# Two PSUM banks in turn for the delta rule's products, and the second head group's v transposed a step ahead

## The chip, the cores and the metric

The program runs on one core of one Trainium2 chip. The metric is the device time of one execution in microseconds (us). A measurement is the median of several runs; lower is better.

## The reference

It is one inference step of a decoder trunk of two layers, for a prompt of 2048 tokens and a group of 8 sample rows, in fp32. The even layer is attention beside pooling; the odd layer is a gated delta rule of 6 heads beside a spatial gate, and only its prompt part is touched here. The 2048 tokens are cut into chunks; a state s of 128x128 per head goes from chunk to chunk:

```python
def step(s, xs):
    q_c, k_c, u_c, w_c, g_c, a_c = xs
    delta = u_c - jnp.einsum('bhcd,bhdv->bhcv', w_c, s)
    o = jnp.einsum('bhcd,bhdv->bhcv', q_c * jnp.exp(g_c)[..., None], s) + jnp.einsum('bhij,bhjv->bhiv', a_c, delta)
    g_last = g_c[..., -1:]
    s = s * jnp.exp(g_last)[..., None] + jnp.einsum('bhcd,bhcv->bhdv', k_c * jnp.exp(g_last - g_c)[..., None], delta)
    return s, o
```

Here `u_c` and `w_c` come from v and k through the inverse of a triangular matrix of each chunk. The outputs are the two residual streams and the new caches and states.

## The kernel before

The odd layer works on two halves of 1024 tokens. In each half the main flow is made of matmul blocks: the input projection with its convolution (`conv_silu`, PSUM tiles cv), the gates and the output projection (`out_tile`, tiles acc). A large product is made as three matmuls in fp32r (`mm3`, L193 to L195: high by high, low by high, high by low). The delta rule of a half is a generator, `delta`; the main flow calls `tick` between its blocks, and each tick writes some more of the recurrence into the program at a high priority. The Tile framework's scheduler then sets the order on each engine by operands, buffers and priority. This order is fixed in the program: an engine works its own list from the top.

A half has 8 chunks of 128 tokens by 2 head groups (g = 0 and 1, three heads each), that is 16 items. Each item goes through stages with the lags of `DORD` (L50): load (q, k and the decay row gb), front (transposes of k and q, decay matrix A, products of k and q; L1338 to L1368), and then, per chunk with both groups together, blocks (inverse of 16x16 blocks on VectorE, with small loads and stores), merge16 and merge (inverses merged up to the matrix U of 128x128 a head; merge16 also loads v, L1434). Then comes step (L1497), which is the recurrence, and out (the output is transposed and stored).

The step of an item with state S is, by line:

- L1508: three transposes of v by TensorE; L1509: VectorE multiplies them by s, giving vt.
- L1512: ScalarE makes Sd, the decayed S.
- L1515: p1 = k·S; L1517: VectorE makes r = vt − p1.
- L1520: p2 = U·r; L1522: VectorE makes e from it.
- L1525 and L1526: output po = q·S + A·e. L1529: p3 = k·e; L1530: VectorE writes S = Sd + p3.
- L1533 to L1536: o is normalised (squares on ScalarE, power on GpSimd, multiplication on VectorE); L1544 to L1547: o is transposed, copied and stored.

PSUM has eight banks. `bank()` (L81) gives each product a tile of the kind that it names, and `OD` (L55) lists the banks that a kind takes in turn: the step's v transposes, p1, p2 and p3 are of kind rr (bank A); po is do, the output's transposes are oo (both bank B); front's products and the sample's are fr and side (bank C); the merges are dm (the two buffers Y). acc and cv use X (two buffers), X and D in the main. A product waits until the tile that held its bank before has been read.

```python
OD = dict(acc="XXD", fr="C", dm="Y", rr="A", do="B", oo="B", side="C", gv0="XXDYYAB", gv1="XXD", cv0="XXDYYAB", cv1="XXD")
```

All DMAs are issued by SyncE. In the second half the sample's own delta rule is mixed into the same stretch (L1575 to L1662). The run ends with the output projection of the last token tile, which needs the last item's o.

Of the kernel before, what the change touches and what calls it, by code (L numbers as in the profile page):

```python
# [15 lines left out]
ALU = mybir.AluOpType  # L16
# [4 lines left out]
P = 128  # L21
# [30 lines left out]
CM = 1  # L52
BQ, QB, GB, AB = 1, 5, 1, 4
PRIO = dict(delta=1000)
OD = dict(acc="XXD", fr="C", dm="Y", rr="A", do="B", oo="B", side="C", gv0="XXDYYAB", gv1="XXD", cv0="XXDYYAB", cv1="XXD")  # L55
PB, TB = 9, 6
W0 = 4, 4, 2
WT = 0
# [5 lines left out]
class Net:  # L64
# [1017 lines left out]
    def odd(self):  # L1082
        nc, I, O = self.nc, self.I, self.O
        st = ExitStack()
        self.banks = dict(OD, h=OD["acc"])
        self.odd_consts(st)
# [199 lines left out]
    def delta(self, half, gt, dl):  # L1286

        pairs = [dict(half=half, t=t) for t in range(8)]
        items = [dict(half=half, t=t, g=g, pair=pairs[t]) for t in range(8) for g in range(2)]
        stages = dict(load=self.delta_load, front=self.delta_front, blocks=self.delta_blocks, merge16=self.delta_merge16,  # L1290
                      merge=self.delta_merge, step=self.delta_step, out=self.delta_out)
        for i in range(len(items) + 6):

            for j, lag in DORD:
                if 0 <= i - lag < len(items):
                    x = items[i - lag]
                    pair = j in ("blocks", "merge16", "merge")
                    if not pair or x["g"]:
                        stages[j](x["pair"] if pair else x, gt, dl)
                        if j != "load":  # L1300
                            yield
# [156 lines left out]
    def delta_merge(self, y, gt, dl):  # L1458
# [31 lines left out]
        for x in y["gs"]:  # L1490
# [3 lines left out]
                mm(pu[:H, i, :], xx[H:, i, :H], U[H:, i, H:], start=True, stop=True)  # L1494
            nc.scalar.mul(U[:H, :, H:], pu[:H], -1.0)

    def delta_step(self, x, gt, dl):  # L1497

        nc = self.nc
        mm = nc.tensor.matmul  # L1500
        k, q, kt, A, U = (x[n] for n in ("k", "q", "kt", "A", "U"))
        g, c0 = x["g"], x["c0"]
        S = self.S[g]
        b3 = lambda a: a[:, :, None].broadcast_to([P, 3, P])
        v, vt = x["v"], self.d3(dl, "vt", 2)
        pt = self.bank("rr", 3, P)
        for i in range(3):
            nc.tensor.transpose(pt[:, i, :], v[:, i, :], self.ident)  # L1508
        nc.vector.tensor_tensor(vt, pt, b3(x["s"]), ALU.mult)  # L1509
        Sd = self.d3(dl, "Sd", 2)  # L1510
        for i in range(3):
            nc.scalar.mul(Sd[:, i, :], S[:, i, :], x["el"][:, i:i + 1])  # L1512
        p1 = self.bank("rr", 3, P)
        for i in range(3):
            mm(p1[:, i, :], k[:, i, :], S[:, i, :], start=True, stop=True)  # L1515
        r = self.d3(dl, "re", BR)
        nc.vector.tensor_tensor(r, vt, p1, ALU.subtract)  # L1517
        p2 = self.bank("rr", 3, P)
        for i in range(3):
            mm(p2[:, i, :], U[:, i, :], r[:, i, :], start=True, stop=True)  # L1520
        e = self.d3(dl, "re", BR)
        nc.vector.tensor_tensor(e, p2, b3(x["c"]), ALU.mult)  # L1522
        po = self.bank("do", 3, P)
        for i in range(3):
            mm(po[:, i, :], q[:, i, :], S[:, i, :], start=True, stop=False)  # L1525
            mm(po[:, i, :], A[:, i, :], e[:, i, :], start=False, stop=True)  # L1526
        p3 = self.bank("rr", 3, P)
        for i in range(3):
            mm(p3[:, i, :], kt[:, i, :], e[:, i, :], start=True, stop=True)  # L1529
        nc.vector.tensor_tensor(S, Sd, p3, ALU.add)  # L1530
        o, ss = self.d3(dl, "o", BO), dl.tile([P, 3], F32, tag="oss", name="oss", bufs=2)
        for i in range(3):
            nc.scalar.activation(o[:, i, :], po[:, i, :], AF.Square, scale=P ** -0.5, accum_out=ss[:, i:i + 1])  # L1533
        nc.vector.tensor_tensor(ss, ss, x["qe"], ALU.add)
        self.rstd(ss, 0.0)
        nc.vector.tensor_tensor(o, po, b3(ss), ALU.mult)  # L1536
        x["o"] = o
# [247 lines left out]
```

## Time and profile before

| | us |
|---|---|
| median of 3 runs | 3079.72 |
| lowest and highest of them | 3072.3, 3086.37 |
| profiled execution | 3071.84 |
| its span in the trace | 3070.1 |
| TensorE (PE) busy | 2787.3 |
| VectorE (DVE) busy | 2083.2 |
| GpSimd (POOL) busy | 1669.2 |
| ScalarE (ACT) busy | 1491.4 |

The profiled execution is one run; its span goes from the first to the last instruction of the trace. PEld is TensorE's weight load, which lies beside its matmuls; SPq is the queue of SyncE that issues the DMAs. The trace names tiles by their names in the program (rr, do, vt), and lines of kernel.py as L1508. PEclk is the granted clock of TensorE as a share of full speed; its mean over the run is 0.966.

### The profile page before, as it was taken

The page shows a single profiled execution, that of the slowest core. Times are in us where ns is not written, and L with a number is a line of the kernel's source. Part 1 is how long each engine was busy: PE and PEld are TensorE (multiplying, and loading weights), DVE is VectorE, ACT ScalarE, POOL GpSimd, SP SyncE. Part 2 cuts the span into 40 slices and gives each one's busy share as a digit, 9 for nine tenths or more (in the row PEclk, how much of TensorE's full clock was granted, in tenths as well). Part 3 has the DMA queues.
Part 4 walks back from the last instruction along what each step waited for, and adds up shares of the span by engine and source line. Part 5 has one row for each costly group of instructions (what it writes and reads, how often), then busy time and mean ns, then how long its engine had stood idle before and what let it go on. Part 6 is the DMA issues. An engine that isn't in the chain of part 4 may idle for free. (4 is left out here: it accounts for less than half of the span.)

```text
span 3070.1 us, 57853 instructions
## 1 busy us (share of the span) xinstructions
PE 2787.3 (91%) x20425; PEld 2534.0 (83%) x20425; DVE 2083.2 (68%) x4067; ACT 1491.4 (49%) x4431; POOL 1669.2 (54%) x1223
## 2 busy tenths in 40 slices
PE   8999899999998889989897988989999888778999
PEld 8999798899777777778787888878989878667887
DVE  5464455554898989894588777567888564567562
ACT  6644245534787778772222324445554533454331
POOL 4576546562567776674576665454444253255541
PEclk9999899999999999999999999999999999999999
DMA  4567866556344333307676665434333333467543
GB/s 162 160 206 245 254 209 200 192 180 181 104 100 110 93 84 100 73 28 237 212 256 201 201 192 179 130 112 139 106 92 97 94 84 113 134 180 219 146 122 99
DMA packets 428062, 462.55 MB, mean 151 GB/s; under 512 B 84988, under 2 KB 338341, under 8 KB 427773
## 3 DMA queue, kind: packets, MB, share of 16 engines
q1 hardware_dynamic: 427772, 458.86, 50.3%
q8 instruction: 162, 2.65, 0.4%
q14 instruction: 128, 1.04, 0.1%
HBM read 332.41 MB, written 126.33 MB: 149 GB/s over the span
## 5 line engine op out<-in xcount | busy, mean ns | idle before, releaser
L193 PE MATMUL acc<-bh,whi 128*128 128x256 f32 (+4 forms) x1208 | 405.2, 336 | 11.2 <-DVE cx L1244 4.6
L195 PE MATMUL acc<-bh,wlo 128*128 128x256 f32 (+4 forms) x1208 | 402.5, 334 | 3.7 <-DVE wlo L901 3.4
L194 PE MATMUL acc<-bl,whi 128*128 128x256 f32 (+4 forms) x1208 | 402.1, 333 | 2.0 <-DVE bl L882 2.0
L822 ACT ACTIVATE p<-sc,nb 128x512 f32<-128x512 f32 (+3 forms) x480 | 302.1, 642 | 76.0 <-DVE nb L821 63.7
L845 POOL TENSOR_TENSOR p<-p,cf 128x512 f32<-128x512 f32 (+3 forms) x240 | 236.9, 1006 | 182.4 <-ACT p L822 46.4
L635 POOL TENSOR_TENSOR kp<-kp,at 128x768 f32<-128x768 f32 x120 | 207.9, 1741 | 163.6 <-DMA kp<-in_cache_v 145.6
L821 DVE TENSOR_REDUCE nb<-sc 128x1 f32<-128x512 f32 (+3 forms) x480 | 275.6, 597 | 19.4 <-PE sc L820 10.3
L195 PE MATMUL cv<-bh,wlo 128*128 128x346 f32 (+2 forms) x864 | 283.6, 329 | 3.2 <-POOL wlo L174 2.3
L193 PE MATMUL cv<-bh,whi 128*128 128x346 f32 (+2 forms) x864 | 284.3, 329 | 1.4 <-DVE th L429 1.0
L194 PE MATMUL cv<-bl,whi 128*128 128x346 f32 (+2 forms) x864 | 284.4, 329 | 0.0
L174 POOL TENSOR_TENSOR wlo<-wraw,whi 128x1024 fp32r<-128x1024 f32 (+1 forms) x90 | 216.7, 2411 | 117.3 <-ACT whi L172 117.1
L557 POOL TENSOR_TENSOR kp<-kp,qb 128x768 f32<-128x768 f32 x88 | 167.3, 1907 | 180.0 <-DMA kp<-in_cache_k 137.6
L193 PEld LDWEIGHTS acc<-bh,whi 128*128 128x128 f32 (+1 forms) x1208 | 231.6, 192 | 27.8 <-issue 5.6
L193 PE MATMUL acc<-whi,bh 128*128 128x256 f32 x864 | 250.6, 290 | 0.2 <-DVE th L425 0.2
L194 PE MATMUL acc<-wlo,bh 128*128 128x256 f32 x864 | 249.2, 289 | 1.4 <-POOL wlo L174 1.4
L195 PE MATMUL acc<-whi,bl 128*128 128x256 f32 x864 | 249.0, 288 | 0.0
L195 PEld LDWEIGHTS acc<-bh,wlo 128*128 128x128 f32 (+1 forms) x1208 | 231.4, 192 | 20.4 <-DVE wlo L901 4.6
L194 PEld LDWEIGHTS acc<-bl,whi 128*128 128x128 f32 (+1 forms) x1208 | 231.4, 192 | 15.7 <-DVE bl L882 2.5
L859 PE MATMUL pv<-v,pt 128*128 128x128 f32 x1632 | 218.1, 281 | 16.7 <-ACT pt L857 9.8
L817 PE MATMUL sc<-kh,q 128*128 128x512 f32 (+2 forms) x480 | 210.0, 438 | 25.1 <-ACT p L822 21.0
L859 PEld LDWEIGHTS pv<-v,pt 128*128 128x128 f32 x1632 | 201.3, 194 | 31.4 <-ACT junk L862 13.9
L637 DVE TENSOR_TENSOR sacc<-sacc,kp 128x768 f32<-128x768 f32 x120 | 176.0, 1467 | 73.6 <-POOL kp L635 64.8
(445 smaller groups left out, 8449.8 us busy)
## 6 DMA issues: line engine op xcount, KB each, us to landing
kp<-in_cache_k SPq DMA_DIRECT2D x128, 384.0 KB
kp<-in_cache_v SPq DMA_DIRECT2D x128, 384.0 KB
wraw<-in_w_in_e SPq DMA_DIRECT2D x56, 512.0 KB
wraw<-in_w_in_o SPq DMA_DIRECT2D x56, 512.0 KB
mc<-cat SPq DMA_DIRECT2D x72, 256.0 KB
mg<-sg SPq DMA_DIRECT2D x72, 256.0 KB
kh<-kh SPq DMA_DIRECT2D x48, 256.0 KB
kl<-kl SPq DMA_DIRECT2D x48, 256.0 KB
```

Source lines behind the costliest of these rows:

```text
L174: e.tensor_tensor(lo, raw, hi.bitcast(F32), ALU.subtract)
L193: mm(out, ah, bh, start=first, stop=False)
L194: mm(out, ah, bl, start=False, stop=False)
L195: mm(out, al, bh, start=False, stop=last)
L557: (nc.vector if j % 3 == 2 else nc.gpsimd).tensor_tensor(k, k, qb, ALU.mult)
L635: nc.gpsimd.tensor_tensor(h3(w), h3(v), self.at[:, b, j, :, None].broadcast_to([P, NH, P]), ALU.mult)
L637: nc.vector.tensor_tensor(acc, acc, v, ALU.add)
L817: mm(sc[:, :w], qc, kh[:, c, :w], start=True, stop=False)
L821: nc.vector.tensor_reduce(nb[:, c, j:j + 1], sc[:, :n], AX.X, ALU.max, negate=True)
L822: nc.scalar.activation(p[:, c, :n], sc[:, :n], AF.Exp, bias=nb[:, c, j:j + 1], accum_out=l[:, c, j:j + 1])
L845: nc.gpsimd.tensor_tensor(p[:, 1, :n], p[:, 1, :n], cf[:, 1, j:j + 1].broadcast_to([P, n]), ALU.mult)
L859: mm(pv, tt[:, t, :], kvt[j][2][:, t, :], start=j == 0 and t == 0, stop=j * 4 + t == nk - 1)
```

## The change

The kind rr takes the banks A and Y in turn, so p1, p2 and p3 of the steps alternate between A and one of the two buffers that the merges use. The transposes of v and the multiplication that makes vt become a function of their own, `delta_v`, with a kind of its own on bank C. Each item knows the next one; after a step has written S, it calls `delta_v` for the next item if that item's v is loaded. Since merge16 loads v for both groups of a chunk together, this is so for the step of group 0 (the next item is group 1 of the same chunk); group 0 of the next chunk still makes its vt at the head of its own step.

```diff
-OD = dict(acc="XXD", fr="C", dm="Y", rr="A", do="B", oo="B", side="C", gv0="XXDYYAB", gv1="XXD", cv0="XXDYYAB", cv1="XXD")
+OD = dict(acc="XXD", fr="C", dm="Y", rr="AY", vt="C", do="B", oo="B", side="C", gv0="XXDYYAB", gv1="XXD", cv0="XXDYYAB", cv1="XXD")
...
+        for x, y in zip(items, items[1:] + [{}]):
+            x["next"] = y
...
+    def delta_v(self, x, dl):
+
+        nc = self.nc
+        x["vt"] = vt = self.d3(dl, "vt", 2)
+        pt = self.bank("vt", 3, P)
+        for i in range(3):
+            nc.tensor.transpose(pt[:, i, :], x["v"][:, i, :], self.ident)
+        nc.vector.tensor_tensor(vt, pt, x["s"][:, :, None].broadcast_to([P, 3, P]), ALU.mult)
+
     def delta_step(self, x, gt, dl):
...
-        v, vt = x["v"], self.d3(dl, "vt", 2)
-        pt = self.bank("rr", 3, P)
-        for i in range(3):
-            nc.tensor.transpose(pt[:, i, :], v[:, i, :], self.ident)
-        nc.vector.tensor_tensor(vt, pt, b3(x["s"]), ALU.mult)
+        if "vt" not in x:
+            self.delta_v(x, dl)
+        vt = x["vt"]
...
         nc.vector.tensor_tensor(S, Sd, p3, ALU.add)
+        if "v" in x["next"]:
+            self.delta_v(x["next"], dl)
```

In the changed file the lines have other numbers: v transposes L1505, p1 L1524, q·S L1534, A·e L1535, p3 L1538, output transposes L1555; merge16's first product is L1442 instead of L1440, the q transposes L1357 instead of L1355.

The first place is TensorE's order in the first half, at the step of a second head group. S_20770 and S_20771 are the states of the two groups; T and cm are operands of merge16. Before:

```order
L1440 MATMUL dm<-T,cm 128x128 x3
L1355 MATMUL fr<-ident,qk 128x128 x3
L193 MATMUL cv_27911<-bh,whi 128x352
L194 MATMUL cv_27911<-bl,whi 128x352
L195 MATMUL cv_27911<-bh,wlo 128x352
L193 MATMUL cv_27911<-bh,whi 128x352
L1526 MATMUL do<-re,A 128x128
L1525 MATMUL do<-S_20771,qk 128x128
```

Now:

```order
L195 MATMUL cv_27995<-bh,wlo 128x346
L1538 MATMUL rr<-re,kt 128x128 x3
L1524 MATMUL rr<-S_20770,qk 128x128 x3
L1534 MATMUL do<-S_20771,qk 128x128
L1535 MATMUL do<-re,A 128x128
L193 MATMUL fr<-qh 128x256
L194 MATMUL fr<-cm,qh 128x256
L195 MATMUL fr<-qh,cm 128x256
```

The product p3, which came behind q·S and A·e, now stands ahead of them, with p1 of the next group right behind it; the merge's product, which came ahead of them, now follows 48 rows later.

The second place is TensorE's order at the start of the second half's recurrence, at its first transposes of q. Before:

```order
L195 MATMUL cv_30322<-bh,wlo 128x346
L1355 MATMUL fr<-ident,qk 128x128 x3
L1508 MATMUL rr<-ident,v 128x128 x3
L193 MATMUL cv_30322<-bh,whi 128x346
L194 MATMUL cv_30322<-bl,whi 128x346
```

Now, where the front stage's products of that item stand:

```order
L195 MATMUL cv_30356<-bh,wlo 128x352
L193 MATMUL fr<-qh 128x256
L194 MATMUL fr<-cm,qh 128x256
L195 MATMUL fr<-qh,cm 128x256
```

The v transposes have left this place for one 674 matmuls later; the first instruction here that needs another engine's work is then the product of the front stage, 39 matmuls behind where the v transposes were.

The third place is the end of TensorE's order, at the last output transposes. Before:

```order
L195 MATMUL acc<-bh,wlo 128x512
L193 MATMUL acc<-bh,whi 128x512
L1544 MATMUL oo<-ident,o 128x128 x3
L194 MATMUL acc<-bl,whi 128x512
L195 MATMUL acc<-bh,wlo 128x512
```

Now:

```order
L194 MATMUL acc<-bl,whi 128x256
L195 MATMUL acc<-bh,wlo 128x256
L1555 MATMUL oo<-ident,o 128x128 x3
L193 MATMUL acc<-bh,whi 128x256
L194 MATMUL acc<-bl,whi 128x256
L195 MATMUL acc<-bh,wlo 128x256
```

They moved 23 matmuls towards the end of the order: 30 instead of 53 are left between them and the first product of the last tile.

## Rows read from the trace of the kernel before

**Rows 1.** the page's busy time of each engine: us, share of the span, instructions

```profile
PE 2787.3 (91%) x20425; PEld 2534.0 (83%) x20425; DVE 2083.2 (68%) x4067; ACT 1491.4 (49%) x4431; POOL 1669.2 (54%) x1223
```

**Rows 2.** windows; columns: us, PE, PEld, DVE, ACT, POOL busy, PEclk, DMA share, GB/s

```profile
2100.00:2435.00 335.00, 324.14 (x2778) 306.79 (x2779) 260.89 (x639) 178.56 (x563) 150.62 (x114) 1.00 0.34 102
2435.00:2455.00 20.00, 10.46 (x58) 10.18 (x57) 7.90 (x21) 7.37 (x27) 2.84 (x3) 0.75 0.50 130
2500.00:2550.00 50.00, 32.03 (x208) 26.92 (x209) 26.72 (x62) 9.91 (x23) 32.31 (x17) 0.76 0.31 62
2625.00:2720.00 95.00, 68.58 (x470) 59.86 (x470) 49.38 (x122) 40.53 (x148) 39.41 (x25) 0.92 0.55 149
```

**Rows 3.** PE's waits, 1935 to 3071: awaited line, us in total, times, longest

```profile
PE side L1599 <- DVE arena L1596: 11.0, 1, 11.0
PE rr L1508 <- DMA v<-y: 9.5, 1, 9.5
...
PE rr L1508 <- DVE S L1530: 6.8, 5, 2.5
PE rr L1515 <- DVE vt L1509: 6.8, 4, 4.0
...
PE oo L1544 <- DVE o L1536: 4.5, 5, 1.7
...
PE do L1526 <- DVE re L1522: 3.0, 2, 2.6
```

**Rows 4.** groups of instructions, whole run: busy us, mean ns | idle before, releaser

```profile
L1509 DVE TENSOR_TENSOR vt<-rr,ks 128x384 f32<-128x384 f32 x32 | 17.5, 546 | 2.1 <-PE rr L1508 2.1
...
L1508 PE MATMUL rr<-ident,v 128*128 128x128 f32 x96 | 17.0, 283 | 16.5 <-DMA v<-y 9.5 <-DVE S L1530 6.8
```

**Rows 5.** PE's waits, 2625 to 2720

```profile
PE rr L1515 <- DVE vt L1509: 5.4, 2, 4.0
...
PE rr L1508 <- DVE S L1530: 2.5, 1, 2.5
```

**Rows 6.** DVE's waits, 2625 to 2720

```profile
DVE s L1647 <- DMA s<-sdd: 32.8, 10, 6.0
```

**Rows 7.** timeline at the stall of 2441: start us, us, instruction [idle before, releaser]

```profile
2439.73 0.32 PE L193 MATMUL cv<-bh,whi 128*128 128x346 f32 x1
...
2440.21 0.31 PE L193 MATMUL cv<-bh,whi 128*128 128x346 f32 x1
...
2441.16 0.49 PE L1355 MATMUL fr<-ident,qk 128*128 128x128 f32 x3
...
2447.43 0.37 SPq L1434 DMA_DIRECT2D v<-y  x1
...
2450.70 1.00 POOL L1338 TENSOR_TENSOR A<-gb,dmask 128x384 f32<-128x384 f32 x1 [15.65 <-DMA gb<-grow]
...
2451.18 0.90 PE L1508 MATMUL rr<-ident,v 128*128 128x128 f32 x3 [9.54 <-DMA v<-y]
...
2451.74 0.98 ACT L1340 ACTIVATE A<-A,nG 128x128 f32<-128x128 f32 x3 [10.26 <-POOL A L1338]
...
2454.93 0.20 ACT L1357 ACTIVATION_READ_ACCUMULATOR N<-fr 128x1 f32 x1
```

**Rows 8.** timeline and chain of waits at the end of the run

```profile
3039.22 0.56 DVE L1536 TENSOR_TENSOR o<-do,oss 128x384 f32<-128x384 f32 x1 [0.96 <-POOL oss L126]
...
3044.31 0.49 PE L1544 MATMUL oo<-ident,o 128*128 128x128 f32 x3
...
3045.50 2.15 DMA cat<-o
...
3053.62 0.50 PE L193 MATMUL acc<-bh,whi 128*128 128x512 f32 x1 [1.98 <-ACT whi L900]
...
3058.54 0.12 PE acc L194
...
3058.78 0.23 PE acc L193
```

## The prediction

> **What bounds the kernel now.** I read the page first, then the windows of the second half of the run, then TensorE's waits there, then the timeline of the two longest stalls, and last the chain that ends the run. The page says TensorE: it is busy 2787.3 us, 91% of the span, and no other engine passes 2083.2 [rows 1]. The delta recurrence, the only code that is changed, runs from about 1935 us on, so only that part can give anything back. The windows [rows 2] show it in two kinds. In the long stretch 2100 to 2435 TensorE is busy 324.14 of 335.00 us at a granted clock of 1.00: all its idle time together is 10.9 us. Holes stand at 2435 to 2455 (10.46 of 20.00 busy, clock 0.75), 2500 to 2550 (32.03 of 50.00, clock 0.76) and 2625 to 2720 (68.58 of 95.00, clock 0.92).
>
> What TensorE waits for in that part [rows 3] divides into what the change can reach and what it cannot. It can reach the v transposes waiting for bank A (they wait for S, because the group before still holds the bank: 6.8 us in 5 waits), k·S waiting for vt (6.8 us in 4), and one wait of the v transposes for the load of v (9.5 us). It cannot reach the longest wait of all, 11.0 us of the sample's own matmuls on DVE. That makes 6.8 + 6.8 + 9.5 = 23.1 us, 0.8% of the run, as everything that stands in front of the changed instructions today.
>
> **The change, part by part.**
>
> *Work.* The count stays: 32 steps with three transposes of v each (96 matmuls, 283 ns each) and one multiplication by s (32 of 546 ns) [rows 4]. Nothing is added on TensorE, DVE or a queue, so this costs nothing by itself. The results go to the front stage's bank C in place of A. On GpSimd nothing moves past anything. On SP the loads of v keep their place; only one small load of the block stage stands behind a store, and nothing waits for it at once. I take 0, with the 2.15 us of one store [rows 8] as the upper bound and nothing below.
>
> *The wait for S behind the v transposes.* For the second head group the transposes now stand ahead of the group before, on another bank; for the first group they stand on C too. So the 6.8 us of waits for S go, but 2.5 of them lie at 2625 to 2720 [rows 5]. There the recurrence is mixed with the sample's state updates, and DVE, which must make vt, e and S in its own order, waits 32.8 us in 10 waits for loads of the sample's state [rows 6]. Taking a bank wait out ahead of that leaves the next instruction waiting for the same DVE. I count 6.8 − 2.5 = 4.3 us as gained.
>
> *The wait for vt behind k·S.* 6.8 us in 4 waits, but 5.4 of them in that same stretch [rows 3, 5], and with the same reason they move on. I count 1.4 us.
>
> *The hole at 2441.* After the q transposes at 2441.16 TensorE stands for 9.54 us in front of the v transposes; their load was issued at 2447.43 [rows 7]. In the changed order the first v transposes of this half stand 674 matmuls later, so this wait goes. What is late next? TensorE goes on with 39 products of the convolution at 0.16 us each (three of them between 2439.73 and 2440.21) and then comes to the products of the front stage, which write bank C over the q transposes. ScalarE must read those first, and its reads stand in its queue behind the exponentials of A, which wait for GpSimd's A at 2450.70 (1.00 us), itself 15.65 us behind a load. ScalarE starts the exponentials at 2451.74 and ends its last read at 2455.13 [rows 7]; that chain is untouched by the change. So TensorE stops at about 2441.65 + 39 × 0.16 = 2447.9 and stays until the chain is done, which also runs the other small reads of the front stage: to about 2455.6, by my estimate from these rows. The stall is then 7.7 us in place of 9.5: a gain of about 2. The bounds are nothing and the whole 9.5 us, plus at most 0.25 × 20.00 = 5.0 us of clock, since the window was granted 0.75 [rows 2]. I take 2, by the rows of ScalarE.
>
> *The pair of banks.* The recurrence now alternates between A and the two buffers Y that the merges use. That takes away waits of one product for the read-out of the one before, but it adds two. A merge product that takes a Y buffer stands behind the read of S of the second group; and S may not be overwritten before q·S has read it, while q·S needs bank B, which the output transposes of the group before still hold. Neither wait is in the trace in that form. The nearest rows are the output transposes waiting for o (4.5 us in 5 waits, longest 1.7) and the product of e waiting for its operand (3.0 in 2) [rows 3]. Spread over all 32 steps the first is 4.5 / 32 = 0.14 us. If every one of 32 steps paid the mean of a wait, 4.5 / 5 = 0.9 us, it were 28.8 us. Below nothing: 4.5 + 3.0 us, if a quicker recurrence takes these waits away as well. I take 0.14 for each of the 16 steps of the second group, 2.2 us lost, since in 2100 to 2435 TensorE has matmuls of the convolution and the gates to do meanwhile and the merges' operands come early.
>
> *The end.* The run's last chain goes from the last S and o through the last output transposes, the store and the load of the mixed tile to the last product [rows 8]. o is ready at 3039.22 + 0.56, but TensorE, in its fixed order, comes to the transposes only at 3044.31: their place in the order, not o, sets the start. In the changed order they stand 23 matmuls later (with 30 and not 53 left until the wait for the last tile). Five of these have 512 columns at 0.23 us and 18 have 256 at 0.12 [rows 8]: 5 × 0.23 + 18 × 0.12 = 3.3 us later, all of it on the path, since after it TensorE waits for that chain in both (1.98 us for ScalarE's weights there). I count 3.3 lost.
>
> *Sum.* −4.3 − 1.4 − 2.0 + 2.2 + 3.3 = −2.2 us. Against the profiled execution's own 3071.84 that is 3069.6. That execution was 7.9 us under the median 3079.72 of the three runs, so I forecast **3077 us**. About 0.5% (15.4 us) is what a measurement of this kernel can tell from no change, so this is no change.
>
> **Rivals.**
>
> *Faster: all waits on the changed path go, and nothing takes their place.* 6.8 + 6.8 + 9.5 and 5.0 of clock, less 3.3 at the end: −24.8 us, 3055 by the median. For it: the recurrence is one serial chain, the order now puts three more independent matmuls ahead of it, and the waits are seen. Against it: the two places with the largest share have their next wait already in the rows [rows 6, 7]. The Trainium skill, Perfetto Trace Analysis, Matmuls, says that independent groups of matmuls should rotate through several PSUM banks so that reading one overlaps the next one's products. By that rule this rival would hold; the trace agrees only so far that the waits on bank A exist, and they are 13.6 us without the load of v [rows 3]. 0.24.
>
> *Slower: bank B becomes the loop's end.* p3 of the second group now stands ahead of q·S, and S waits for q·S, which waits for the chain squares, power, o, output transposes, copy on bank B. If each of the 16 second steps lost (0.9 + 1.7) / 2 = 1.3 us, the mean between the mean and the longest wait for o [rows 3], the sum were −4.4 + 16 × 1.3 = +16.4 us, that is 3096. It decides from 1.25 us a step on, where the loss passes 15.4 + 4.4. For it: the output transposes already wait for o. Against it: TensorE has other work in the order between. 0.12.
>
> *Slower: the clock.* The granted clock stays 1.00 over 2100 to 2435 although TensorE makes short waits there, and is below 0.8 only in windows with a stall of 9.5 and 11.0 us [rows 2, 3]. If the new alternation makes many short gaps in that stretch and the grant fell to 0.95 of full speed, 335 × 0.05 = 17 us more, 3079.7 − 2.2 + 17 = 3094. The Trainium skill, TensorE: Matmul & The Clock Gate, A second HAM failure mode, tells of a kernel that cycled through PSUM banks each iteration, whose small gaps made the clock swing between its levels; it speaks against this change. The trace does not bear it out: no row at 2100 to 2435 shows a fall. 0.04.
>
> *It does not do what it says.* The scheduler sets the order from operands; were the chain left in place, the time would stay at 3080. The order shows it moved. 0.02, and same.
>
> **How the numbers follow.** Forecast 0.58, faster rival 0.24, bank B 0.12, clock 0.04, nothing moved 0.02. Faster by over 0.5% means below 3064: 0.24. Slower: 0.12 + 0.04 = 0.16. Within: 0.58 + 0.02 = 0.60. The range goes from 3047, the fast rival with the waits for o and e (7.5 us) gone too, to 3100, the bank B rival with 1.5 us a step in place of 1.3 (+16 × 0.2 = 3.2). Beyond lie the far bound of bank B, 28.8, with no gain beside it, and holes I did not see.
>
> **What would show it.** In the profile after, no wait of the v transposes for S or for the load of v; TensorE stopped from about 2448 to 2456 before a product of the front stage in place of the 9.54 us; the waits at 2625 to 2720 renamed but about as long; the last output transposes 3 us later against the end of the products before them. Wrong would be: new waits of the products q·S or of the merges that add up to over 15 us (bank B or Y), a granted clock below 1.00 in the long stretch, or an end of the half that comes some 20 us sooner (the faster rival).

## The result and the profile after

The change makes the kernel slower: 3110.01 us median (3106.93 to 3114.5) against 3080.53 before on the same chips, a ratio of 1.0095 with a 95% interval of 1.0074 to 1.0116, some 29 us. The forecast was 3077 us, no change; the measured time lies above its range.

The profiled execution has a span of 3109.9 us against 3070.1. That is 39.8 us, some 10 more than the medians lie apart: the profiled execution before, 3071.84 us, was a quick one of its kernel. The engines have the same instructions in the same number, but TensorE is busy 12.6 us longer and VectorE 14.8; the line of the page that answers to [rows 1] is this one:

```profile
PE 2799.9 (90%) x20425; PEld 2548.5 (82%) x20425; DVE 2098.0 (67%) x4067; ACT 1489.4 (48%) x4431; POOL 1667.6 (54%) x1223
```

To see where the time went, I took instructions of the main flow that both traces have, in the same number, on DVE, ACT and POOL, and read how much later each of them comes. Up to 1930 us, where TensorE's order is still the same in both, the run is already 5 us later, which is no work of the change. From 2130 to 2440 it loses 19 us more, from 2620 to 2810 6 us, and in the last 110 us some 11 us; of the stretches between, 2440 to 2620 gives back 6 us and 2810 to 2960 loses 6. In the second half neighbouring instructions differ by up to 10 us in how late they come, so there these figures are rough. The windows of these three stretches, of the kernel before (columns as in [rows 2]):

```profile
2130.00:2440.00 310.00, 301.73 (x2583) 286.18 (x2583) 238.46 (x600) 163.22 (x527) 130.52 (x99) 1.00 0.33 97
2620.00:2810.00 190.00, 150.70 (x1114) 129.13 (x1110) 114.84 (x260) 83.54 (x278) 86.19 (x60) 0.91 0.63 175
2960.00:3070.10 110.10, 103.41 (x798) 89.09 (x796) 36.59 (x87) 18.74 (x64) 18.30 (x18) 1.00 0.36 107
```

and of the same stretches of the program after:

```profile
2134.00:2463.00 329.00, 310.21 (x2653) 295.51 (x2653) 251.39 (x617) 164.59 (x540) 136.43 (x107) 0.97 0.32 93
2637.00:2833.00 196.00, 153.33 (x1051) 136.10 (x1050) 105.50 (x250) 80.40 (x263) 80.28 (x59) 0.83 0.62 170
2989.00:3109.90 120.90, 110.46 (x927) 95.45 (x925) 47.53 (x108) 24.92 (x92) 27.16 (x23) 0.98 0.32 94
```

In the first stretch TensorE's idle time rises from 310.00 − 301.73 = 8.3 us to 329.00 − 310.21 = 18.8, so 10.5 of the 19 us are waits. The other 8.5 are busy time. The granted clock falls from 1.00 to 0.97, which is worth at most 0.03 × 329 = 10 us; but there are also 70 more matmuls in the stretch (x2653 against x2583; short products of the merges above all), so what the clock alone cost is not shown. In the second the waits grow by 3.4 us (39.3 to 42.7) and the busy time by 2.6, with 63 matmuls fewer and the clock at 0.83 in place of 0.91. In the last the waits grow by 3.7 us, and 129 matmuls more are still to be done in it (x927 against x798): work that comes late. TensorE's waits from 1940 us on, of the kernel after:

```profile
PE side L1610 <- DVE arena L1607: 13.2, 1, 13.2
PE dm L1496 <- ACT xx L1494: 7.1, 2, 6.3
PE fr L193 <- ACT N L1359: 7.0, 1, 7.0
...
PE dm L1471 <- DVE U L1458: 6.7, 10, 1.9
...
PE fr L1350 <- issue: 5.8, 2, 3.8
PE rr L1529 <- DVE S L1539: 5.7, 2, 4.6
...
PE oo L1555 <- DVE o L1547: 4.2, 3, 3.2
PE dm L1471 <- DVE qe L1390: 3.9, 1, 3.9
...
PE fr L1350 <- DVE vt L1506: 2.4, 2, 1.5
...
PE do L1534 <- ACT o L1557: 1.2, 1, 1.2
```

The waits of the v transposes for S and for v's load [rows 3] are gone. In their place stand waits of the front stage and of the merges: the k transposes (fr L1350), the merges' first products with N (dm L1471), p2 waiting for S (rr L1529, 5.7 us), and at the start of the second half the front's products (fr L193 for N, 7.0 us). Only 2.4 us of the front's and the merges' waits name vt, and none of those lies in the first stretch.

### The profile page after: what moved, and what is told of

Same layout as the page of the kernel before. It is cut to its first block, busy times and chain, and to the rows that moved or that the text cites. A ratio compares the mean times of both kernels' runs of the same rounds, so it can differ in the third digit from the quotient of the medians.

```text
span 3109.9 us, 57878 instructions
## 1 busy us (share of the span) xinstructions
PE 2799.9 (90%) x20425; PEld 2548.5 (82%) x20425; DVE 2098.0 (67%) x4067; ACT 1489.4 (48%) x4431; POOL 1667.6 (54%) x1223
## 5 line engine op out<-in xcount | busy, mean ns | idle before, releaser
L193 PE MATMUL acc<-bh,whi 128*128 128x256 f32 (+4 forms) x1208 | 406.7, 337 | 19.6 <-DVE dd L1218 6.9
L193 PE MATMUL cv<-bh,whi 128*128 128x346 f32 (+2 forms) x864 | 286.1, 331 | 4.1 <-DVE th L429 2.5
L174 POOL TENSOR_TENSOR wlo<-wraw,whi 128x1024 fp32r<-128x1024 f32 (+1 forms) x90 | 218.7, 2434 | 106.2 <-ACT whi L172 106.0
L193 PEld LDWEIGHTS acc<-bh,whi 128*128 128x128 f32 (+1 forms) x1208 | 233.1, 193 | 36.3 <-DVE dd L1218 7.1
L193 PE MATMUL acc<-whi,bh 128*128 128x256 f32 x864 | 250.1, 290 | 0.2 <-DVE th L425 0.2
L637 DVE TENSOR_TENSOR sacc<-sacc,kp 128x768 f32<-128x768 f32 x120 | 169.6, 1413 | 81.6 <-POOL kp L635 72.9
```

The costliest lines, as they stand in the source:

```text
L174: e.tensor_tensor(lo, raw, hi.bitcast(F32), ALU.subtract)
L193: mm(out, ah, bh, start=first, stop=False)
L637: nc.vector.tensor_tensor(acc, acc, v, ALU.add)
```

## The experiments

Three parts were changed at once: the bank of the v transposes, the look-ahead (v transposed a step ahead), and the two banks for p1, p2 and p3. All ratios are against the kernel before, run on the same chip beside them, with a 95% interval; runs that differ in the chip are compared by their ratios.

| run | v transposes on | ahead | products on | ratio |
|---|---|---|---|---|
| the change | C | yes | A, Y | 1.0095 (1.0074 to 1.0116) |
| look_a | C | yes | A | 1.0131 (1.0111 to 1.0151) |
| c_only | C | no | A | 1.0114 (1.0086 to 1.0143) |
| pair_c_nolook | C | no | A, Y | 1.0069 (1.0052 to 1.0087) |
| vt_a | A | yes | A | 0.9996 (0.998 to 1.0013) |
| pair_vt_a | A | yes | A, Y | 1.0003 (0.9984 to 1.0022) |
| pair_vt_a_nolook | A | no | A, Y | 1.0038 (1.0024 to 1.0051) |
| pair_only | A | no | A, Y | 1.008 (1.0058 to 1.0101) |
| vt_b | B | yes | A | 1.0059 (1.0043 to 1.0075) |
| pair_vt_b | B | yes | A, Y | 1.0101 (1.0079 to 1.0122) |
| pair_vt_d | D | yes | A, Y | 1.0154 (1.0127 to 1.0182) |

The parts do not add up: with v on C the two banks in turn take time off (1.0131 to 1.0095, and 1.0114 to 1.0069 without the look-ahead), with v on A and no look-ahead they cost.

**First four runs: one part at a time.** Theory Y: sharing the merges' banks Y costs the time. Theory C: the v transposes on the front stage's bank C cost it. Theory D: any new order of these instructions costs, since the order before happened to fit.

look_a, from the changed kernel (of the line of `OD`, here and below, only the kinds that differ):

```diff
-rr="AY", vt="C"
+rr="A", vt="C"
```

> The look-ahead alone: v transposes on bank C, one step ahead for the second head group, but the recurrence products all on bank A again. Theory Y (the merges' banks shared with the recurrence cost the time): 3075 to 3085 us, as before the change, ratio to before 0.998 to 1.002, and the granted clock is back at 1.00 in the stretch 2130 to 2420. Theory C (the transposes of v on the front stage's bank cost it): 3100 to 3115. Theory D (any new order of these instructions costs, through VectorE's and GpSimd's order): between 3090 and 3115 here too.

Measured 3129.16 us, worse than the whole change and above every range expected. As the account of the whole change, theory Y falls: without the shared Y the loss is larger, not smaller.

pair_only, from the kernel before:

```diff
-rr="A"
+rr="AY"
```

> The two banks A and Y in turn alone, with the v transposes on the same kind at the head of their own step as before. Theory Y: 3100 to 3115 us (ratio 1.007 to 1.012). Theory C: 3075 to 3085. Theory D: 3090 to 3115.

Measured 3111.39 us, as theory Y had it for this run. So it is not theory C alone: this kernel puts nothing of v on C and loses 0.8%. It is taken up again below.

c_only, from the changed kernel: rr="A", and the two lines that call `delta_v` for the next item are removed.

> The v transposes on bank C at the head of their own step, no look-ahead, recurrence products on A. Theory Y: 3075 to 3085 us. Theory C: 3095 to 3115, since the transposes stand in front of the front stage's in bank C. Theory D: 3090 to 3115.

Measured 3123.51 us, above the range of theory C: v transposes on C at their old place in the program, and nothing else, cost 1.1%.

pair_c_nolook, from the changed kernel: the same two lines are removed.

> Both banks A and Y in turn and the v transposes on bank C, without the look-ahead. Theory Y: 3100 to 3115 us, as the whole change. Theory C: 3100 to 3115. If the look-ahead itself cost the time: 3075 to 3085.

Measured 3109.08 us. So the look-ahead is not what costs here. All four lose, which left C and D standing.

**Where, and by what.** half0_only and half1_only have the whole change in one half of the tokens only (kinds rr and vt of their own for each half):

```diff
-        pt = self.bank("vt", 3, P)
+        pt = self.bank("vt0" if x["half"] == 0 else "rr1", 3, P)
...
-        if "v" in x["next"]:
+        if x["half"] == 0 and "v" in x["next"]:
```

> The whole change, but in the first half's recurrence alone; the second half's is as before. From the trace of the changed kernel the stretch 2130 to 2440 lost 19 us and the later ones 16. If the losses belong to the places: this one 3095 to 3103 us, with the stretch 2620 to 2810 and the end as before. Theory D (any new order costs in all of it): the same 3095 to 3110, but with the loss spread to the second half too.

> The whole change in the second half's recurrence alone. If the losses belong to the places: 3093 to 3103 us, with 2130 to 2440 as before at a granted clock of 1.00, and the half-speed time in the sample's stretch and the wait before the last tile (5 to 9 us) as in the whole change. If the first half's loss is what matters: 3078 to 3088.

Measured 3099.71 us, ratio 1.0051 (1.0032 to 1.0071), and 3113.99 us, 1.0103 (1.0064 to 1.0141). Both halves lose, and together (1.5%) more than the whole change does, so the two losses do not add up either. The stretch 2130 to 2440 of the kernel before, in half0_only:

```profile
2133.00:2462.00 329.00, 310.55 (x2655) 295.61 (x2654) 251.65 (x617) 164.31 (x539) 136.25 (x107) 0.97 0.32 93
```

and in half1_only:

```profile
2136.00:2447.00 311.00, 302.64 (x2584) 286.40 (x2582) 240.39 (x600) 163.39 (x527) 130.04 (x99) 1.00 0.33 96
```

The first half's loss, 329 in place of 310 us with the clock at 0.97, is there whole when only the first half is changed, and not there when only the second is. As expected, half0_only loses little behind that stretch: it is 22 us late at 2440 and 28.6 at the end. half1_only was above the expected 3093 to 3103. In its own profiled execution, its quickest, with a span of 3100.9 us against 3070.1, the stretch 2620 to 2810 takes some 10 us more and the end some 18 us more, both as rough as above.

p3_first tests theory D with a new order and the old banks: in the kernel before, the three lines of p3 are written ahead of the output products.

> The kernel before with one statement moved: p3 is written ahead of the output products, all banks as before. Nothing depends on it but the order. Theory D (a new order costs by itself, whatever it is for): 3095 to 3115 us. If the banks' new couplings cost the time: 3078 to 3088.

Measured 3087.24 us, ratio 1.002 (1.0 to 1.0039). This new order costs little, which speaks against theory D. It is one other order and no more: early_a below, with nothing of v on C, loses 0.5%, so that orders differ in cost without bank C is not ruled out.

pair_vt_a is the whole change with one letter changed back:

```diff
-rr="AY", vt="C"
+rr="AY", vt="A"
```

> The whole change, with the v transposes on bank A in place of the front stage's C. The order shows the merges of the second half within 50 matmuls of where they stand before the change, against 60 to 90 later in the whole change. If bank C costs (the front stage, and by it the blocks and the merges, fall behind): 3075 to 3090 us. If the shared merge banks cost: 3100 to 3115.

Measured 3085.79 us, ratio 1.0003. The loss is gone with bank C, and the two banks in turn stay. The same stretch, of pair_vt_a:

```profile
2141.00:2447.00 306.00, 298.97 (x2592) 285.62 (x2587) 236.94 (x599) 161.11 (x518) 130.28 (x99) 1.00 0.33 98
```

It takes 306 us, at a clock of 1.00. The move to bank C can be read off three pairs of runs that differ in that letter or in that alone: 1.0003 and 1.0095, 0.9996 and 1.0131 (vt_a and look_a), and the kernel before and 1.0114 (c_only). In the fourth pair, two banks in turn without the look-ahead, it is less: 1.0038 and 1.0069, whose intervals just miss each other.

**Theory L, from the traces.** `bank()` asks for its tiles in the order in which the program is written, and the tiles of one bank follow each other in that order, as in a ring. On C the tiles of vt now stand between those of the front stage: the step of an item is written ahead of the front of the item four later. So those k transposes cannot start before vt has been read, and vt cannot be made before the front's products of the item ahead of them have been read. DVE's and PE's rows of the kernel after show it:

```profile
2091.86 0.28 DVE L1369 TENSOR_TENSOR A<-fr,A 128x128 f32<-128x128 f32 x1
...
2094.74 0.49 PE L1505 MATMUL vt<-ident,v 128*128 128x128 f32 x3
...
2096.61 0.55 DVE L1506 TENSOR_TENSOR vt<-vt,ks 128x384 f32<-128x384 f32 x1
...
2098.83 0.49 PE L1505 MATMUL vt<-ident,v 128*128 128x128 f32 x3
...
2100.76 0.56 DVE L1506 TENSOR_TENSOR vt<-vt,ks 128x384 f32<-128x384 f32 x1
...
2103.46 0.49 PE L1350 MATMUL fr<-ident,qk 128*128 128x128 f32 x3
```

Front's last read, v of one group, its read, v of the other, its read, k of the next front: one after the other. In the kernel before, the v of the first of these two groups is read 36 us earlier (the two traces lie at most some 5 us apart there), behind S and ahead of the same reads of the front. DVE's rows:

```profile
2055.99 0.56 DVE L1530 TENSOR_TENSOR S<-Sd,rr 128x384 f32<-128x384 f32 x1 [1.04 <-PE rr L1529]
2060.82 0.55 DVE L1509 TENSOR_TENSOR vt<-rr,ks 128x384 f32<-128x384 f32 x1
...
2077.68 0.29 DVE L1367 TENSOR_TENSOR A<-fr,A 128x128 f32<-128x128 f32 x1
```

From the starts and ends of such rows, over the 32 steps (medians, us; the first two columns count from the last such instruction that has ended when vt starts; merge16 counts from the start of its mask product on GpSimd, L1426 before, to vt of its first group; the last column is the mean distance per item between the k transposes' first reads of items 4 and 15 of the first half):

```
                 vt starts after    vt starts after      from merge16   from vt's end    us per item
                 the last S         front's last read    to its vt      to next k read   of the front
before           4.2                19.0                 14.7           15.8             26.7
vt_a             4.2                18.8                 16.1           14.8             26.8
pair_vt_a        4.0                22.6                 11.3           15.7             26.9
the change       31.4                7.7                 29.3            8.2             27.3
c_only           14.0                4.6                 36.3            4.1             29.0
vt_b              9.7               23.5                 25.6            7.4             27.4
```

With vt on A it follows the S of the step before by 4 us whatever the front does. On C it follows the front's last read, and the k transposes follow it. By theory L that holds back the front, and behind it the blocks and merges. The last two columns alone do not single out C: in vt_b, which puts nothing of v on the front's bank, they are 7.4 and 27.4. And the chain from the ring to the waits is argued, not shown: in the first stretch the two longest waits of the kernel after (dm L1471 3.9 us, fr L1350 3.8, together 7.7 of the 10.5 more) come behind VectorE instructions that ran beside GpSimd's for many times their usual length (1.80 and 1.83 us for L1386 and L1388 with medians of 0.17, 5.13 for L1254 with 0.52). Another order with v on C might miss these meetings; no run shows it.

**Runs made from theory L.** vt_a is the look-ahead alone, all on A (rr="A", vt="A" in the changed kernel); pair_vt_a_nolook is pair_vt_a without the two lines of the look-ahead.

> The look-ahead alone, on bank A, with all products on A. Its order on TensorE is nearly that of the kernel before. Theory L: no change, 3075 to 3088 us, against 3129 for the look-ahead with the transposes on bank C. If the look-ahead itself cost: 3100 and more.

> The run pair_vt_a without the look-ahead: v transposes at the head of their own step on bank A, products on A and Y in turn. If the look-ahead is what made the pair free of cost there: 3095 to 3110 us. If the pair costs only in the pattern in which p1 and p3 of every step lie on Y (the run with the pair alone): 3080 to 3090.

Measured 3083.44 us, ratio 0.9996: on A the look-ahead costs nothing, and gains nothing. It can gain nothing there, since the v transposes still wait for the bank. TensorE's waits of vt_a from 1940 us on are those of [rows 3]:

```profile
PE vt L1505 <- DMA v<-y: 8.8, 1, 8.8
PE rr L1524 <- DVE vt L1506: 8.2, 3, 3.9
PE vt L1505 <- DVE S L1539: 7.6, 5, 3.3
```

And 3096.33 us, 1.0038: within the first expectation, at its lower end. With v on A the look-ahead makes up some of what the pair costs, and pair_only's 1.008 has another part. There p1 and p3 of every step lie on Y, v and p2 on A. From the front's last read to merge16 it takes 35.2 us (median of 16, from rows as above) against 22.3 before, which agrees with the merges being held by the step on Y; no run takes that apart, so it stays open.

early_a and early_pair_a move `delta_v` into merge16, for both groups, with three buffers for vt:

```diff
+        for x in y["gs"]:
+            self.delta_v(x, dl)
         for x in y["gs"]:
             U, T, xx = x["U"], x["T"], x["xx"]
```

> v transposed right after its load in the merge16 stage, for both head groups, on bank A; the recurrence products on A alone, bank C left to the front stage. Theory L (tiles of one bank are handed out in the order of the program, so what shares the front's bank holds the front stage to the pace of the step): nothing shares C, so no loss, and the waits of the step for v's transposes go: 3068 to 3085 us, ratio 0.995 to 1.001. If any early transposing costs: 3095 to 3115.

> As early_a, with the recurrence products on A and Y in turn as in the change. Theory L: 3068 to 3088 us. If the two banks cost by themselves, as the run with the pair alone suggests (0.8%): 3095 to 3110.

Measured 3100.82 us, ratio 1.0053 (1.0033 to 1.0072), and 3102.23 us, also 1.0053 (1.0035 to 1.0071). Both missed theory L's range and lie in the other: earlier is not better even on A. TensorE's waits of early_a from 1936 us on:

```profile
PE vt L1507 <- DMA v<-y: 7.9, 2, 7.4
PE vt L1507 <- DVE S L1541: 7.5, 4, 2.7
```

The v transposes stand again at their load and at S, 15.4 us in all against 16.3 in [rows 3], which tells why nothing is won, not where 17 us are lost. Theory L itself does not give the low expectation when the ring of A is looked at too: `merge16` is written between two steps, so on A its tiles of v stand between products of other steps, which do not depend on them but must wait for their load. The waits of p2 and A·e for VectorE grew from 4.1 us to 13.1; what else costs there was not taken apart.

The last three runs ask whether any bank but A costs as much, or C because of who shares it: vt="B" with rr="A" (vt_b) and with rr="AY" (pair_vt_b), and vt="D" (pair_vt_d).

> The look-ahead with the v transposes on bank B (output products and output transposes), recurrence products on A. Theory L: the front stage is free, so at most the step itself is held: 3080 to 3098 us, ratio up to 1.005. Any bank but A costs: 3110 to 3130, as with C.

> The whole change with the v transposes on bank B in place of C. Theory L: 3080 to 3100 us. Any bank but A costs: 3105 to 3120.

> The whole change with the v transposes on bank D, which the blocks of the main flow take every third time. Theory L: now the main flow is held to the step's pace, TensorE waits in acc and cv blocks: 3100 us and more. Any bank but A costs: 3105 to 3120 too; the waits in the trace tell, blocks of the main flow waiting for vt only under L.

Measured 3103.54 us (1.0059), 3114.29 (1.0101) and 3129.58 (1.0154). vt_b lies between the two expectations, 5.5 us above theory L's; pair_vt_b is 14 us above theory L's and within "any bank but A costs"; pair_vt_d is in theory L's and above the other. The waits speak for L. In vt_b:

```profile
PE oo L1555 <- DVE vt L1506: 12.6, 5, 4.4
...
PE do L1534 <- DVE vt L1506: 5.8, 1, 5.8
```

and in pair_vt_d:

```profile
PE vt L1505 <- DVE vt L1506: 6.6, 4, 4.5
...
PE vt L1505 <- DVE clast L1247: 3.1, 1, 3.1
...
PE acc L193 <- DVE vt L1506: 1.6, 2, 1.3
```

On B the output products and output transposes, which share that bank, wait for vt; on D a block of the main flow (acc) waits for vt, and v waits for a block of the convolution (clast). So on each bank waits appear between v and whoever shares it, and the output stage of B is not harmless. They are not the price: in pair_vt_d 1.6 us of the main flow's waits name vt, and it lost 46 us. On A the neighbours in the ring are p3 of the step before and p1 of the same step, and vt stands between those two in any case. That A is free for this reason is argued from the waits and the table; no run gave vt a bank that nobody else uses, since all eight are taken.

No version beat the kernel before; vt_a and pair_vt_a equal it.

## Why the prediction was wrong

**The step that failed** is the first of the change's parts: "The results go to the front stage's bank C in place of A", with "I take 0". The move was costed as work, and on its own bank's busy time, not as an order that it forces between two stages. Taking that one step back (pair_vt_a) takes the time back from 1.0095 to 1.0003, some 28 us; making that step alone (c_only) gives 1.0114. The bound, one store of 2.15 us, was no bound: it took no account of 32 tiles in the ring of the front. The sign of the sum depended on it. In the same paragraph "On GpSimd nothing moves past anything" was wrong too: by the traces over 130 of its 1223 instructions have another place in its order, the first at 1993 us, where A (L1338) came ahead of wlo (L174) and now comes behind it; the long VectorE instructions above ran beside GpSimd's.

**The waits for S and vt** behave as forecast: both are gone [rows 3], and in the sample's stretch they came back under another name, p2 waiting 5.7 us for S. What they are worth shows in pair_vt_a, from 1940 us on:

```profile
PE vt L1505 <- DMA v<-y: 10.4, 2, 9.2
...
PE vt L1505 <- DVE S L1539: 1.7, 1, 1.7
PE rr L1524 <- DVE vt L1506: 1.6, 2, 1.2
```

The 13.6 us of waits for S and vt are down to 3.3, and the time is 1.0003. By its interval no more than 0.16%, 5 us, can have been won. The forecast of a few us agrees with that, and the fast rival's 13.6 us for these waits do not. Its other part, the load of v and the clock, was not tried without bank C: the load is still waited for here. The rule of the Trainium skill, Perfetto Trace Analysis, Matmuls, quoted for that rival, gave no time here: pair_vt_a rotates, at 1.0003.

**The hole at 2441** was right, mechanism and size. The forecast was a stop before a front product of 7.7 us in place of 9.54, for ScalarE's reads behind the exponentials of A. (By the traces the v transposes themselves stand 808 matmuls later, not 674; nothing hangs on it.) The timeline after has:

```profile
2477.57 0.58 PE L193 MATMUL fr<-qh 128*128 128x256 f32 x1 [7.03 <-ACT N L1359]
```

**The end** was right in its wait: 3.3 us were forecast. TensorE's wait before the last tile is

```profile
3092.66 0.80 PE L193 MATMUL acc<-bh,whi 128*128 128x512 f32 x1 [5.28 <-ACT whi L900]
```

against 1.98 [rows 8], and 5.28 − 1.98 = 3.3. But the window from 2960 on lost some 11 us, not 3.3. Its other part is not a wait at the last tile: 120.90 − 110.46 = 10.4 us idle in it against 6.7 before, and a clock of 0.98, so most is busy time, 110.46 us against 103.41, for the 129 matmuls that come late.

**The pair of banks** was given 2.2 us, with a far bound of 28.8. In pair_vt_a the whole is 1.0003, which agrees, but an interval of 0.2% to either side cannot tell 2.2 us from nothing. That it fits is partly luck: without the look-ahead the same pair costs 0.4% (pair_vt_a_nolook) and 0.8% (pair_only), and with v on C it gains. The slow rival of bank B named 3096 us and the output stage as the place; the measured sign was that rival's, but the mechanism was another: the wait of q·S for the copy of o is 1.2 us in one wait in the trace after, and the output transposes wait 4.2 us for o in place of 4.5 [rows 3]. Nor did the merges' waits reach the 15 us that the prediction named as a sign: those before dm products grew from 18.7 us to 26.1.

**The clock rival** was half right. The granted clock did fall in the long stretch, by 0.03, where 0.05 was named. But not from the alternation: pair_vt_a alternates the same banks and keeps 1.00. It fell behind waits that stand there with v on C (the change, half0_only) and not with v on A. The windows around one of them, of the kernel after:

```profile
2160.00:2180.00 20.00, 20.00 (x148) 19.68 (x147) 18.87 (x55) 10.34 (x38) 5.55 (x4) 1.00 0.29 96
2180.00:2200.00 20.00, 14.66 (x133) 13.37 (x132) 13.25 (x29) 10.70 (x38) 13.95 (x13) 0.95 0.23 60
2200.00:2220.00 20.00, 19.99 (x174) 18.82 (x174) 16.08 (x33) 7.94 (x21) 3.69 (x2) 0.88 0.39 115
2220.00:2240.00 20.00, 20.00 (x151) 19.86 (x151) 18.27 (x51) 10.09 (x38) 8.64 (x8) 1.00 0.33 90
```

TensorE stands for 5.3 us between 2180 and 2200, 3.90 of them in front of the merge product L1471, and is granted part of the next 20 us at the lower level, 1.2 GHz, although it is busy throughout. So behind 5.3 us of standing come up to 0.12 × 20 = 2.4 us for the clock. What the Trainium skill, TensorE: Matmul & The Clock Gate, A second HAM failure mode, tells of cycling banks, these runs do not show of cycling alone.

## What to carry to other kernels

Where a pool hands out the tiles of a bank in the order of the program, putting a product on a bank ties it to everything else on that bank: it waits for the reader of the tile ahead of it, and the stage behind it waits for its own. Before moving a product, name its new neighbours in that ring, and ask whether it depends on them anyway; if not, price the move by how far apart the two stages ran before, not by its work. And a wait of TensorE in a stretch that ran at full clock can cost more than its length (here up to 2.4 us behind 5.3); the short ones of the kernel before, 8.3 us in all from 2130 to 2440, left the clock at 1.00.

## What the runs showed of the hardware

One VectorE instruction ran as long as several GpSimd instructions beside it, and seems to have been held by them. In the kernel after, VectorE's rows at 2240:

```profile
2240.35 5.13 DVE L1254 SCALAR_TENSOR_TENSOR cth<-cth,cx 128x340 f32<-128x340 f32 x1 [0.22 <-ACT cth L1253]
2245.41 0.28 DVE L1369 TENSOR_TENSOR A<-fr,A 128x128 f32<-128x128 f32 x1
```

and GpSimd's, without a gap between them:

```profile
2240.42 1.02 POOL L1433 TENSOR_TENSOR T<-ucp,bmask 128x384 f32<-128x384 f32 x1
2241.41 1.00 POOL L1433 TENSOR_TENSOR U<-ucp,bmask 128x384 f32<-128x384 f32 x1
2242.37 1.79 POOL L1428 TENSOR_TENSOR cm<-N,lmask 128x768 f32<-128x768 f32 x1
2244.13 0.98 POOL L1340 TENSOR_TENSOR A<-gb,dmask 128x384 f32<-128x384 f32 x1
```

That instruction takes 0.68 us on the average of the kernel before (group L1254, 54 of them) and 0.84 after. Here it took 5.13 and ended 0.4 us behind GpSimd's run. The read of bank C behind it (A<-fr, 2245.41) came late by that, and the k transposes, in front of which TensorE stood 3.84 us (3.8 in the waits above), followed at 2245.78. The Trainium skill, SBUF — State Buffer, SBUF: two separate sides, says that a VectorE instruction with two inputs in SBUF and a GpSimd instruction that reads SBUF share a pair of ports, which the one that starts first holds for its whole length. The rows agree, and if that is the cause, the one that waits can lose several turns in a row. No run here changed GpSimd's part, so the cause is not shown.
